# Two of three partial products in one matmul, in the products that end in the residual

## The chip, the core and the metric

The program runs on one core of a Trainium2 chip. The metric is the device time of one execution, from the first to the last instruction and what little lies around them, in microseconds; three timed runs of the kernel before are known.

## The reference, cut to what matters

Two transformer blocks on 256 tokens of width 1024, everything in float32. The first block has two layers, each of a gated FFN, a mixer and another gated FFN; the second block has a hybrid mixer (a recurrence and latent attention), attention to a memory, and an FFN with a convolution. Cut to the statements whose last product ends in the residual `x`:

```python
for l in range(DEPTH):                                   # DEPTH = 2
    x = x + 0.5 * gate * swiglu(adaln_in(x, ...), w1, w3, w2)      # (silu(h @ w1) * (h @ w3)) @ w2, w2: 2752 x 1024
    h = adaln_in(x, ...) @ w_in[l]
    mix = mixer_ab(h, ...) if l % 2 == 0 else mixer_cd(h, ...)
    x = x + gate * (mix @ w_out[l])                      # w_out: 1024 x 1024
    x = x + 0.5 * gate * swiglu(adaln_in(x, ...), w1, w3, w2)
...                                                      # second block: hybrid mixer, then
x = x + memory_attention(...) @ w_mem_o                  # 512 x 1024
x = x + ffn(...) @ w_down                                # 2816 x 1024
```

Each `adaln_in` is a root-mean-square norm of `x` with a gain and a shift that come from a conditioning vector.

## The kernel before, in words

Features lie on partitions: `x` is [128, 8, 256], eight tiles n of 128 features by 256 tokens (T = 256). A float32 product is made of three products in a rounded format (fp32r), as both factors are split into a hi part and a lo part: hi·hi, hi·lo and lo·hi. For one block of 128 by 128 weights that is `mm3` (L649): three matmuls of 256 columns (258 where two columns for the shift are taken along, L1006 and its like), each with its own weight load, the first two with the weights' hi part on the operand's hi and lo part, the third with the weights' lo part on the operand's hi part. All three add up in one half of a PSUM bank.

Weights come as a stream of slabs [128, 1024] in a fixed order (`load_job`, queue of SyncE). ScalarE makes a slab's hi part (`hi_job`), VectorE its lo part (`lo_job`, L586, 128x1024); VectorE also makes the modulation's vectors from slabs of another kind in the same stream (an operation on 128x1024 that the profile calls CUSTOM_DVE_ANT_0, and `order` ISA). Five pairs of buffers hold hi and lo slabs.

`block_mms` (L691) runs through a stream of blocks, all K tiles of one output tile n in a row; it makes the last product of the four gated FFNs (22 K tiles; the 22nd has 64 rows with the hi and lo part in one tile, two matmuls), of the memory attention (4 K tiles) and of the last FFN, `ffn2` (22 K tiles). `slab_mms` (L665) takes a slab for each output tile (8 K tiles); it makes all first products and the mixers' output products. Output tiles rotate over three PSUM banks (`mmr`).

When an output tile is whole, `residual` (L901) runs on VectorE: one operation reads the 256 columns in PSUM, multiplies by the gate (or only adds) and adds to `x[:, n]`; then the bank is free. It also starts what the next norm needs of the tile (`Norm.feed`): ScalarE makes the hi part of gain times x and VectorE the lo part (`scale`), ScalarE squares the tile and VectorE adds the square to a sum (`square`). After the eighth tile two plain matmuls reduce the sum over partitions (`Norm.root`), eight small VectorE operations make the reciprocal root, and two matmuls against the identity spread it to all partitions. Where the next norm has a shift, one small VectorE operation (128x16, `shift_cols`) writes two extra columns of the operand, once the last tile of `x` is done.

The order of instructions on each engine is made while the program is written: `Sched` (L328) keeps a rough clock of every engine from fixed costs and always emits the step that could start first by these clocks; the engines then run strictly in this order. So every operation that is added or made shorter can move others past each other.

Of the kernel before, what the change touches and what calls it, by code (L numbers as in the profile page):

```python
# [12 lines left out]
F32R = mybir.dt.float32r  # L13
# [17 lines left out]
# (name, columns) of the per-channel vectors, one column per tile of 128 channels  # L31
# [17 lines left out]
# square constant matrices [128, 128]  # L49
# [3 lines left out]
def _shape_constants():  # L53
# [14 lines left out]
    # the head that each of 128 rows belongs to: tiles 0-3 hold two heads of 64 rows; tiles 4 and 5 four  # L68
    # heads of 32 rows in the order 0, 2, 1, 3
# [65 lines left out]
# groups of four slabs of the modulation's weights whose products run on the tensor engine, as nothing else does then  # L135
PE_GROUPS = (2,)
# order in which the modulation's nine sections are made
# [163 lines left out]
# how many slabs of the modulation's weights go with each slab of the stream's first stages  # L301
RATES = [(43, 0.55), (65, 0.7), (91, 0.5), (156, 0.31), (199, 0.5), (221, 0.75), (247, 0.4), (10 ** 6, 0.2)]
STAGES = (65, 91, 156, 221, 247, 312, 343, 351)
# other priorities in a stage of the stream
# [5 lines left out]
# Every engine runs its instructions in the order in which they are emitted. The parts of the program are  # L310
# generators ("jobs") that ask for an engine before each step, for events that other jobs fire and for tiles out of
# rings; the scheduler keeps a rough clock of every engine and always emits the step that can start first.
# [18 lines left out]
class Sched:  # L331
# [16 lines left out]
    # runs a job up to its next wait for an engine, an event or a ring  # L348
# [43 lines left out]
    # early: what an engine does before it waits for the operands  # L392
    def charge(self, e, cost, early=0.0, cols=0.0):
# [9 lines left out]
        if e == "pe":  # L403
            # the tensor engine's clock is full in a window after one in which enough columns left the array
            w = int(s / 3.4133)
            if self.busy.get(w - 1, 0.0) < 3060.0:
                cost *= 2
            for i in range(w, int((s + cost) / 3.4133) + 1):
                part = (min(s + cost, (i + 1) * 3.4133) - max(s, i * 3.4133)) / cost
                self.busy[i] = self.busy.get(i, 0.0) + part * cols  # L410
# [64 lines left out]
def _body(tc, ins, out, ctx, dbg=None):  # L475
# [78 lines left out]
    # a load in the order of the stream: the event fires at the time when it should have arrived  # L554
# [61 lines left out]
    # four slabs of the modulation as a row of 512, then as columns  # L616
# [31 lines left out]

    def mm3(ps, w, c, mh, ml, first, last):  # L649
# [13 lines left out]
    # products of whole slabs (K = 1024, one output tile each) with a shared moving operand. The first slabs go  # L663
    # through the parts of K side by side, as the operand may not be whole yet.
    def slab_mms(n, mh, ml, cols, done, kev, parts=(range(7), (7,)), dst=None, pen=None):  # L665
        s = 0
        while s < n:
            g = min(n, 3) if s == 0 else 1
            held = []
            for pi, part in enumerate(parts):  # L670
                for j in range(g):
# [5 lines left out]
                    for k in part:  # L677
# [6 lines left out]
                        mm3(ps[:, o:o + cols], w, k, mh[:, k, :cols], ml[:, k, :cols], first, last)  # L684
# [5 lines left out]
    # products of a stream of [128, 128] blocks, the K tiles of one output tile in a row  # L690
    def block_mms(outs, mh, ml, done, kev, pen=0.0, both=None):  # L691
        w, t = None, 0
        for n, ks in outs:
            ps, = yield mmr, 1
            for k in ks:
# [6 lines left out]
                if k == both:  # L702
                    for i in range(2):
                        pe.matmul(ps[:, :T], w[i][:, t % 8 * P:t % 8 * P + P], mh[:, k, :T], start=False, stop=(i == 1))
                else:
# [5 lines left out]
    # products with the tokens of the operand on partitions: parts [K tile, slab, first column] of 512 columns  # L711
# [17 lines left out]
    # hi and lo parts of a tile  # L729
# [9 lines left out]
    # r = (s / width + eps) ** -0.5: a seed y from the exponent's bits (within 3.5%), then the polynomial of  # L739
    # a = v y^2 that is 1 / sqrt(a) to 3e-8 there. Its leading factor is taken into v.  # L740
# [27 lines left out]
    # a column per token tile onto all partitions  # L768
# [10 lines left out]
    # the products run on A x (hi and lo parts); the root is multiplied in after them  # L779
    class Norm:  # L780
# [23 lines left out]
        # a tile that is normalised before the products  # L804
# [9 lines left out]
        # after the last use of the root its tile goes back  # L814
# [86 lines left out]
    def residual(n, ps, gate, nx):  # L901
        yield "dve"
        if gate is None:
            dve.tensor_tensor(x[:, n], ps[:, :T], x[:, n], ALU.add)
        else:
            dve.scalar_tensor_tensor(x[:, n], ps[:, :T], gate[:, n:n + 1], x[:, n], ALU.mult, ALU.add)
# [12 lines left out]
    # the root's product and the shift's product of an output tile  # L919
# [11 lines left out]
    def ffn(l, i, nm, nxt):  # L931
        with tc.tile_pool(name=f"ffn{l}{i}", bufs=1) as sp:
            gh = tl(sp, [P, 22, T], F32R)
            gl = tl(sp, [P, 21, T], F32R)
# [4 lines left out]
            # the products themselves if the operand was normalised, else with the root's product  # L939
            def done(s, ps):  # L940
# [10 lines left out]
                if s == 42:  # L951
# [9 lines left out]
                    # the last 64 rows' hi and lo parts share a tile; their weights are there twice  # L961
# [1370 lines left out]
```

## Time and profile before

| | us |
|---|---|
| three timed runs | 1434.87, 1426.93, 1431.79 |
| median | 1431.79 |
| profiled execution, span | 1425.3 |
| TensorE busy, weight loads busy | 1374.9, 1293.0 |
| VectorE busy | 1142.6 |
| ScalarE busy | 777.5 |
| DMA queue q1, share of 16 engines | 64.4% |

Of the profiled execution only the span is given; the median of the timed runs lies 6.5 us above it, the fastest 1.6 us. How to read the page: engines run side by side, so busy times don't add up to the span; matmuls are pipelined, so the time between two starts is what a matmul costs, not its duration; the chain of waits (part 4) says what the end waited for, step by step. Nearly every instruction is issued by one helper (L443), so rows are told apart by shapes and by place in time, not by line.

Places in time (us from the span's start), read from the timeline: last product of the first FFN 188 to 250, of the second 484 to 544, of the third 671 to 732, of the fourth 980 to 1041; output product of the first mixer 329 to 356, of the second 818 to 852; of the memory attention 1218 to 1231; of the last FFN 1358 to 1421.5.

### The profile page before, as it was taken

Reading aid. Unit: us, or ns where it says so; the run is one execution under the profiler, and the core shown is the slowest. Engines: PE = TensorE matmul, PEld = TensorE weight load, DVE = VectorE, ACT = ScalarE, POOL = GpSimd, SP = SyncE. Lnnn points to the kernel's source line nnn. Section 1 sums busy time; section 2 is a strip of 40 time slices with the busy share of each in tenths; the row PEclk is TensorE's granted clock in tenths of the full one; section 3 lists DMA queues with packets and bytes.
Section 4 is the critical chain, followed back from the end, with each engine's and each line's share of the span. In section 5 each row is a group of like instructions: output and inputs, shape, how many; then the busy total and the mean of one; then the engine's idle time right before and its main releaser. Section 6 shows DMA issues by size and latency. Waiting matters only on the chain.

```text
span 1425.3 us, 26961 instructions
## 1 busy us (share of the span) xinstructions
PE 1374.9 (96%) x10726; PEld 1293.0 (91%) x10726; DVE 1142.6 (80%) x2183; ACT 777.5 (55%) x1434; POOL 40.2 (3%) x44
## 2 busy tenths in 40 slices
PE   4899999999999999999999999999999998999998
PEld 1499999878999999999998789999997778999998
DVE  5778788796888777888979879986577978799962
ACT  2365554474555544555446646655455765676642
POOL 5200000000000000000000001000000000000000
PEclk9899999999999999999999999999999999999999
DMA  8679899754777787888984447776643134356671
GB/s 296 220 245 317 282 304 331 240 172 150 246 260 245 241 253 226 294 275 270 345 295 149 155 143 228 225 249 188 194 148 119 61 133 133 104 185 186 186 225 49
DMA packets 84656, 305.26 MB, mean 214 GB/s; under 512 B 9515, under 2 KB 11147, under 8 KB 84274
## 3 DMA queue, kind: packets, MB, share of 16 engines
q1 hardware_dynamic: 83250, 299.31, 64.4%
q0 software_dynamic: 1280, 4.22, 0.8%
q8 instruction: 84, 1.38, 0.4%
q14 instruction: 42, 0.34, 0.1%
HBM read 302.43 MB, written 1.06 MB: 213 GB/s over the span
## 4 chain that ended last, share of the span: by engine, by line
PE 83%; DVE 9%; ACT 4%; DMA 2%; issue 1%; POOL 1%; SPq 0%; ACTq 0%; DVEq 0%; POOLq 0%
PE u L443 83%; DVE u L443 9%; ACT u L443 4%; DMA u<-wst 1%; POOL u L443 1%; DMA u<-x 1%; ACT L443 0%; SPq L556 0%; POOL u L2138 0%; ACTq L443 0%; DVEq L443 0%; DVE u L1642 0%; DVE u L1145 0%; DVE u L1643 0%; DVEq L1145 0%
## 5 line engine op out<-in xcount | busy, mean ns | idle before, releaser
L443 PE MATMUL u<-u,u 128*128 128x258 f32 (+7 forms) x10724 | 1373.8, 292 | 46.6 <-ACT u L443 25.5
L443 PEld LDWEIGHTS u<-u,u 128*128 128x128 f32 (+3 forms) x10724 | 1292.8, 189 | 126.7 <-issue 49.9
L443 ACT ACTIVATE u<-u 128x1024 fp32r<-128x1024 f32 (+6 forms) x1001 | 602.8, 632 | 537.4 <-PE u L443 317.3
L443 DVE TENSOR_TENSOR u<-u,u 128x1024 fp32r<-128x1024 f32 (+5 forms) x1065 | 734.5, 721 | 183.4 <-ACT u L443 92.9
L443 DVE SCALAR_TENSOR_TENSOR u<-u,u,u 128x256 f32<-128x256 f32 (+2 forms) x393 | 185.7, 481 | 63.3 <-PE u L443 32.7
L443 ACT ACTIVATE u<-u,u 128x256 f32<-128x256 f32 (+2 forms) x323 | 165.2, 523 | 84.0 <-DVE u L443 61.6
L443 DVE CUSTOM_DVE_ANT_0 u<-u,u,u 128x1024 f32<-128x1024 f32 x140 | 179.7, 1286 | 4.2 <-ACT u L443 3.6
L443 DVE SCALAR_TENSOR_TENSOR u<-u,u 128x2 f32<-128x2 f32 (+5 forms) x127 | 32.5, 261 | 13.3 <-ACT u L443 5.6
L443 ACT ACTIVATE u<-u,u,u 128x256 f32<-128x256 f32 (+1 forms) x43 | 23.8, 564 | 8.3 <-DVE u L443 5.7
L443 DVE TENSOR_SCALAR u<-u,u 128x256 f32<-128x256 f32 (+1 forms) x80 | 25.9, 370 | 1.0 <-ACT u L443 0.2
L443 DVE TENSOR_SCALAR u<-u 128x2 f32<-128x2 f32 (+9 forms) x82 | 14.9, 184 | 7.4 <-PE u L443 3.8
L443 DVE TENSOR_REDUCE u<-u 128x2 f32<-128x512 f32 x20 | 13.3, 685 | 2.0 <-PE u L443 2.0
L443 ACT ACT_TABLE_LOAD x11 | 14.1, 1283 | 0.9 <-PEq L2309 0.7
L443 POOL TENSOR_TENSOR u<-u,u 128x256 f32<-128x256 f32 (+1 forms) x10 | 14.0, 1405 | 13.3 <-ACT u L443 13.0
L1325 POOL DMA_DIRECT2D u<-rope x1 | 0.6, 556 | 479.7 <-PE u L443 479.7
L443 POOL TENSOR_SCALAR u<-u 64x256 f32<-64x256 f32 (+2 forms) x12 | 12.4, 1036 | 25.0 <-DVE u L443 18.8
L443 DVE DVE_READ_ACCUMULATOR2_ANT u<- 128x1 f32 x156 | 12.7, 82 | 0.0
L443 ACT ACTIVATION_READ_ACCUMULATOR u<-u,u,u 128x1 f32 x40 | 8.1, 204 | 0.0
L443 DVE TENSOR_TENSOR u<-u 128x2 f32<-128x2 f32 (+5 forms) x36 | 6.7, 188 | 0.6
L1139 POOL DMA_DIRECT2D u<-sel x1 | 0.6, 575 | 194.0 <-DMA u<-mst 194.0
L443 DVE CUSTOM_DVE_ANT_0 u<-u,u 128x256 f32<-128x256 f32 x16 | 6.0, 419 | 0.0
L443 DVE TENSOR_TENSOR_SCAN u<-u,u 128x256 f32<-128x256 f32 x8 | 5.5, 682 | 0.0
(35 smaller groups left out, 25.8 us busy)
## 6 DMA issues: line engine op xcount, KB each, us to landing
u<-wst SPq DMA_DIRECT2D x417, 512.0 KB, 4.5
u<-mst SPq DMA_DIRECT2D x144, 512.0 KB, 4.8
u<-u POOLq DMA_DIRECT2D x1, 1536.0 KB, 11.8
u<-x SPq DMA_DIRECT2D x1, 1024.0 KB, 8.6
u<-mem SPq DMA_DIRECT2D x1, 1024.0 KB
u<-lruw POOLq DMA_DIRECT2D x2, 512.0 KB, 4.3
out<-u SPq DMA_DIRECT2D x8, 128.0 KB, 2.7
u<-decay SPq DMA_DIRECT2D x1, 512.0 KB, 9.3
```

The source lines that it names most:

```text
L443: r = f(*args, **kw)
L1139: nc.gpsimd.dma_start(sel, ins["sel6"][:8, :4 * P])
L1325: nc.gpsimd.dma_start(rope, ins["rope"])
```

## The change

Operand tiles of the eight products named above are allocated as one tile that holds hi and lo parts side by side (`parts`). A new `mm3_wide` takes the place of `mm3` there: one matmul of 512 columns has the weights' hi part on the operand's hi and lo parts, and writes both halves of the PSUM bank; a second one of 256 columns adds the weights' lo part on the operand's hi part to the first half. `residual` then adds both halves to `x`, in two operations. The 22nd K tile of the gated FFNs keeps its two matmuls, and the hybrid mixer's output product keeps `mm3`. The lo tile of the gated FFNs has 22 tiles instead of 21. The diff also takes comments out; they are left out here.

```diff
+    joined = {}
+
+    def parts(pool, n, cols=T):
+        t = tl(pool, [P, 2, n, cols], F32R)
+        h, lo = t[:, 0], t[:, 1]
+        joined[id(h)] = t, h
+        return h, lo
+
+    def mm3_wide(ps, w, c, mh, k, first, last):
+        h, lo = w[0][:, c * P:(c + 1) * P], w[1][:, c * P:(c + 1) * P]
+        pe.matmul(ps.rearrange("p (a b) -> p a b", a=2), h, joined[id(mh)][0][:, :, k, :T], start=first, stop=False)
+        pe.matmul(ps[:, :T], lo, mh[:, k, :T], start=False, stop=last)
...
-                        mm3(ps[:, o:o + cols], w, k, mh[:, k, :cols], ml[:, k, :cols], first, last)
+                        if wide:
+                            mm3_wide(ps, w, k, mh, k, first, last)
+                        else:
+                            mm3(ps[:, o:o + cols], w, k, mh[:, k, :cols], ml[:, k, :cols], first, last)
...
+                elif wide:
+                    mm3_wide(ps, w, t % 8, mh, k, k == ks[0], k == ks[-1])
...
-    def residual(n, ps, gate, nx):
+    def residual(n, ps, gate, nx, wide=False):
         yield "dve"
-        if gate is None:
-            dve.tensor_tensor(x[:, n], ps[:, :T], x[:, n], ALU.add)
-        else:
-            dve.scalar_tensor_tensor(x[:, n], ps[:, :T], gate[:, n:n + 1], x[:, n], ALU.mult, ALU.add)
+        for p in (ps[:, :T], ps[:, T:])[:1 + wide]:
+            if gate is None:
+                dve.tensor_tensor(x[:, n], p, x[:, n], ALU.add)
+            else:
+                dve.scalar_tensor_tensor(x[:, n], p, gate[:, n:n + 1], x[:, n], ALU.mult, ALU.add)
+        if gate is not None:
...
-            gh = tl(sp, [P, 22, T], F32R)
-            gl = tl(sp, [P, 21, T], F32R)
+            gh, gl = parts(sp, 22)
...
-                                 lambda n, ps: residual(n, ps, gate, nx), kev, both=21)
+                                 lambda n, ps: residual(n, ps, gate, nx, True), kev, both=21, wide=True)
```

The same two edits (`parts`, and `wide=True` with `residual(..., True)`) stand in both mixers, in the memory attention and in `ffn2`.

What it does to the order on the engines. On TensorE, at the start of the first FFN's last product (u_178 and u_179 are the operand's hi and lo part, u_88 and u_89 a slab's hi and lo part, u_129 a PSUM bank):

```order
 L443 MATMUL u_128<-u_69,u_86 128x258
 L443 MATMUL u_128<-u_68,u_87 128x258
-L443 MATMUL u_129<-u_178,u_88 128x256
-L443 MATMUL u_129<-u_179,u_88 128x256
+L443 MATMUL u_129<-u_178,u_88 128x512
 L443 MATMUL u_129<-u_178,u_89 128x256
```

One row of three goes in each such group; TensorE has 10204 rows before and 9196 after. Nothing else of TensorE's order changes but the places of some reductions and spreads at the ends of the stages. The farthest is at the end of the first mixer, where the reduction of the sum of squares (u_135<-u_65,u_93) stands among the first products of the next FFN (u_68 and u_69 are its operand; u_130, u_128 and u_129 its first three output tiles), before:

```order
L443 MATMUL u_128<-u_68,u_86 128x258
L443 MATMUL u_128<-u_69,u_86 128x258
L443 MATMUL u_128<-u_68,u_87 128x258
L443 MATMUL u_135<-u_65,u_93 128x1 x2
L443 MATMUL u_128<-u_68,u_86 128x258
L443 MATMUL u_128<-u_69,u_86 128x258
L443 MATMUL u_128<-u_68,u_87 128x258
```

and after:

```order
L443 MATMUL u_130<-u_68,u_84 128x258
L443 MATMUL u_130<-u_69,u_84 128x258
L443 MATMUL u_130<-u_68,u_85 128x258
L443 MATMUL u_135<-u_65,u_93 128x1 x2
L443 MATMUL u_130<-u_68,u_84 128x258
L443 MATMUL u_130<-u_69,u_84 128x258
L443 MATMUL u_130<-u_68,u_85 128x258
```

Before, 36 matmuls of the next FFN stand ahead of the reduction (21 into u_130, 15 into u_128); after, 18. In the same way the reduction stands 12 matmuls earlier at the end of the third FFN, 6 earlier at the end of the second mixer, 9 later at the end of the fourth FFN and 15 later at the end of the memory attention. On VectorE at the end of the first mixer (u_67 is x, u_69 and u_68 the next operand's lo and hi part, u_93 the sum of squares, u_121 the gate; the row 128x8x2 writes the shift's columns, the rows 128x1024 make lo slabs), before:

```order
L443 SCALAR_TENSOR_TENSOR u_67<-u_128,u_121,u_67 128x256
L443 SCALAR_TENSOR_TENSOR u_67<-u_129,u_121,u_67 128x256
L443 TENSOR_TENSOR u_69<-u_70,u_68 128x8x2
L443 TENSOR_TENSOR u_87<-u_76,u_86 128x1024
L443 SCALAR_TENSOR_TENSOR u_69<-u_67,u_122,u_68 128x256
L443 TENSOR_TENSOR u_93<-u_93,u_101 128x256
L443 SCALAR_TENSOR_TENSOR u_69<-u_67,u_122,u_68 128x256
L443 TENSOR_TENSOR u_89<-u_80,u_88 128x1024
L443 TENSOR_TENSOR u_93<-u_93,u_102 128x256
L443 TENSOR_TENSOR u_91<-u_81,u_90 128x1024
```

and after:

```order
L443 SCALAR_TENSOR_TENSOR u_67<-u_129,u_121,u_67 128x256 x2
L443 TENSOR_TENSOR u_69<-u_70,u_68 128x8x2
L443 TENSOR_TENSOR u_87<-u_76,u_86 128x1024
L443 SCALAR_TENSOR_TENSOR u_69<-u_67,u_122,u_68 128x256
L443 TENSOR_TENSOR u_93<-u_93,u_94 128x256
L443 SCALAR_TENSOR_TENSOR u_69<-u_67,u_122,u_68 128x256
L443 TENSOR_TENSOR u_93<-u_93,u_101 128x256
L443 SCALAR_TENSOR_TENSOR u_69<-u_67,u_122,u_68 128x256
L443 TENSOR_TENSOR u_93<-u_93,u_102 128x256
L443 TENSOR_TENSOR u_89<-u_80,u_88 128x1024
```

The last residual operation of the stage is a pair, the shift's columns come behind it, and three scales and three additions, in place of two and two, now stand between the shift and the small operations of the root; one of the two lo slabs that stood between them has moved behind the root.

## Rows read from the trace of the kernel before

**Rows 1.** Page: busy time (part 1), granted clock (part 2), chain by engine (part 4)
```profile
PE 1374.9 (96%) x10726; PEld 1293.0 (91%) x10726; DVE 1142.6 (80%) x2183; ACT 777.5 (55%) x1434; POOL 40.2 (3%) x44
...
PEclk9899999999999999999999999999999999999999
...
PE 83%; DVE 9%; ACT 4%; DMA 2%; issue 1%; POOL 1%; SPq 0%; ACTq 0%; DVEq 0%; POOLq 0%
```

**Rows 2.** Groups by form, whole span: count | busy us, mean ns | idle before, releaser
```profile
L443 PE MATMUL u<-u,u 128*128 128x258 f32 x4992 | 628.4, 285 | 11.6 <-DVE u L443 6.2 <-ACT u L443 5.3
L443 PE MATMUL u<-u,u 128*128 128x256 f32 x4976 | 624.9, 287 | 10.8 <-ACT u L443 5.8 <-DVE u L443 4.7
```

**Rows 3.** Timeline of TensorE, four stretches: start us, duration us, instruction, count
```profile
189.73 59.52 PE L443 MATMUL u<-u,u 128*128 128x256 f32 x504
...
489.79 50.44 PE L443 MATMUL u<-u,u 128*128 128x256 f32 x431
...
1221.74 9.52 PE L443 MATMUL u<-u,u 128*128 128x256 f32 x78
...
1357.75 63.74 PE L443 MATMUL u<-u,u 128*128 128x256 f32 x530
```

**Rows 4.** The same view of 512 columns, and their group by form
```profile
1155.38 1.33 PE L443 MATMUL u<-u,u 128*128 128x512 f32 x5
...
L443 PE MATMUL u<-u,u 128*128 128x512 f32 x5 | 1.3, 396 | 0.0
```

**Rows 5.** Timeline of TensorE where one column follows each weight load
```profile
1143.26 1.48 PE L443 MATMUL u<-u,u 128*128 128x1 f32 x12
```

**Rows 6.** Timeline of VectorE, the residual after the first mixer; plain additions later
```profile
341.19 2.26 DVE L443 SCALAR_TENSOR_TENSOR u<-u,u,u 128x256 f32<-128x256 f32 x5 [7.32 <-PE u L443]
...
1226.59 1.08 DVE L443 TENSOR_TENSOR u<-u,u 128x256 f32<-128x256 f32 x3
```

**Rows 7.** Stretches, all engines: PE, PEld, DVE, ACT, POOL busy us, PEclk, DMA share
```profile
188.30:249.80 61.50, 61.50 (x523) 61.33 (x521) 52.92 (x77) 30.17 (x41) 0.00 (x0) 1.00 0.93 324
341.00:357.80 16.80, 15.12 (x129) 14.83 (x127) 14.40 (x27) 11.56 (x21) 0.00 (x0) 1.00 0.45 141
836.90:853.40 16.50, 15.28 (x128) 14.79 (x126) 13.99 (x27) 12.86 (x23) 0.54 (x1) 1.00 0.54 165
...
1221.00:1234.40 13.40, 13.40 (x113) 13.38 (x112) 10.95 (x30) 10.20 (x20) 0.00 (x0) 1.00 0.13 40
```

**Rows 8.** Timeline at the end of the first FFN
```profile
249.88 0.48 DVE L443 SCALAR_TENSOR_TENSOR u<-u,u,u 128x256 f32<-128x256 f32 x1
...
250.28 0.17 DVE L443 TENSOR_TENSOR u<-u,u 128x16 fp32r<-128x16 f32 x1
...
250.50 0.39 PE L443 MATMUL u<-u,u 128*128 128x258 f32 x1 [0.66 <-DVE u L443]
```

**Rows 9.** Timeline at the end of the first mixer
```profile
353.97 0.49 DVE L443 SCALAR_TENSOR_TENSOR u<-u,u,u 128x256 fp32r<-128x256 f32 x1 [1.70 <-ACT u L443]
...
357.05 0.87 DVE L443 SCALAR_TENSOR_TENSOR u<-u,u,u 128x256 f32<-128x256 f32 x2
...
357.83 1.30 DVE L443 TENSOR_TENSOR u<-u,u 128x16 fp32r<-128x16 f32 x2
...
358.06 0.39 PE L443 MATMUL u<-u,u 128*128 128x258 f32 x1 [1.94 <-DVE u L443]
```

**Rows 10.** The same, VectorE behind it; TensorE by form in 362.3 to 362.9
```profile
360.18 2.69 DVE L443 TENSOR_TENSOR u<-u,u 128x1024 fp32r<-128x1024 f32 x3
362.88 0.16 DVE L443 TENSOR_SCALAR u<-u 128x2 f32<-128x2 f32 x1
...
L443 PE MATMUL u<-u,u 128*128 128x1 f32 x4 | 0.5, 230 | 0.0
```

**Rows 11.** Timeline at the end of the second mixer
```profile
852.31 0.48 DVE L443 SCALAR_TENSOR_TENSOR u<-u,u,u 128x256 fp32r<-128x256 f32 x1 [1.50 <-ACT u L443]
...
853.66 0.39 PE L443 MATMUL u<-u,u 128*128 128x258 f32 x1 [0.53 <-DVE u L443]
...
855.05 0.42 DVE L443 TENSOR_TENSOR u<-u,u 128x256 f32<-128x256 f32 x1
...
856.72 0.16 DVE L443 TENSOR_SCALAR u<-u 128x2 f32<-128x2 f32 x1
```

**Rows 12.** Timeline at the end of the fourth FFN
```profile
1042.52 0.42 DVE L443 TENSOR_TENSOR u<-u,u 128x256 f32<-128x256 f32 x1
...
1042.99 0.38 PE L443 MATMUL u<-u,u 128*128 128x1 f32 x2 [0.71 <-DVE u L443]
```

**Rows 13.** Timeline, the last tile
```profile
1421.52 0.42 DVE L443 TENSOR_TENSOR u<-u,u 128x256 f32<-128x256 f32 x1 [7.49 <-PE u L443]
1421.97 0.33 SPq L917 DMA_DIRECT2D out<-u  x1
```

More of the change, by code (lines that the diff above doesn't have):

```diff
@@ L661, in take, with slab_mms @@
         return hl_t.pop(i)
-    def slab_mms(n, mh, ml, cols, done, kev, parts=(range(7), (7,)), dst=None, pen=None):
+    def slab_mms(n, mh, ml, cols, done, kev, parts=(range(7), (7,)), dst=None, pen=None, wide=False):
         s = 0
@@ L688, in slab_mms, with block_mms @@
             s += g
-    def block_mms(outs, mh, ml, done, kev, pen=0.0, both=None):
+    def block_mms(outs, mh, ml, done, kev, pen=0.0, both=None, wide=False):
         w, t = None, 0
@@ L1126, in mixer_ab @@
         with tc.tile_pool(name="ab", bufs=1) as sp:
-            mh = tl(sp, [P, 8, T], F32R)
-            ml = tl(sp, [P, 8, T], F32R)
+            mh, ml = parts(sp, 8)
             kev = [Event() for _ in range(8)]
@@ L1300, in mixer_ab @@
             nx = yield from nxt()
-            yield from slab_mms(8, mh, ml, T, lambda n, ps: residual(n, ps, gate, nx), kev,
+            yield from slab_mms(8, mh, ml, T, lambda n, ps: residual(n, ps, gate, nx, True), kev, wide=True,
                                 parts=((4, 5, 6, 7, 0, 1, 2), (3,)))
@@ L1308, in mixer_cd @@
         with tc.tile_pool(name="cd", bufs=1) as sp:
-            mh = tl(sp, [P, 8, T], F32R)
-            ml = tl(sp, [P, 8, T], F32R)
+            mh, ml = parts(sp, 8)
             kev = [Event() for _ in range(8)]
@@ L1502, in mixer_cd @@
             nx = yield from nxt()
-            yield from slab_mms(8, mh, ml, T, lambda n, ps: residual(n, ps, gate, nx), kev,
+            yield from slab_mms(8, mh, ml, T, lambda n, ps: residual(n, ps, gate, nx, True), kev, wide=True,
                                 parts=((0, 1, 2, 3), (4, 5, 6), (7,)))
@@ L1979, in memory_attention @@
             q4 = [tl(sp, [P, T]) for _ in range(4)]
-            oh = tl(sp, [P, 4, T], F32R)
-            ol = tl(sp, [P, 4, T], F32R)
+            oh, ol = parts(sp, 4)
             prs, pts = ring(sp, 4, [P, 2 * T]), ring(sp, 4, [P, 2, T])
@@ L2067, in memory_attention @@
             yield from block_mms([(n, range(4)) for n in range(8)], oh, ol,
-                                 lambda n, ps: residual(n, ps, None, nx), kev)
+                                 lambda n, ps: residual(n, ps, None, nx, True), kev, wide=True)
             put(sm, nm.cols)
@@ L2073, in ffn2 @@
         with tc.tile_pool(name="ffn2", bufs=1) as sp:
-            gh = tl(sp, [P, 22, T], F32R)
-            gl = tl(sp, [P, 22, T], F32R)
+            gh, gl = parts(sp, 22)
             up = ring(sp, 4, [P, T + 2])
@@ L2113, in last @@
             def last(n, ps):
-                yield from residual(n, ps, None, None)
+                yield from residual(n, ps, None, None, True)
                 fin.append(n)
@@ L2119, in ffn2 @@
             all_out = Event()
-            yield from block_mms([(n, range(22)) for n in range(8)], gh, gl, last, kev)
+            yield from block_mms([(n, range(22)) for n in range(8)], gh, gl, last, kev, wide=True)
             yield all_out
```

## The prediction

> **What bounds the kernel now.** I read first the page's busy times, its row of granted clocks and its sums along the chain of waits [rows 1]. TensorE is busy 96% of the span, 83% of the chain is its own work and 9% VectorE's; the clock is granted at the upper of its two levels in nearly every slice. So a microsecond counts if it is on TensorE, or if it is one for which TensorE waits.
>
> Next I read the groups by form [rows 2]. A mean of 285 to 287 ns is a duration, and matmuls overlap; what one costs is the time from start to start. The timeline gives that for unbroken rows of matmuls [rows 3]: less one overlap (0.28 us, the mean duration), divided by the count less one. The last product of the first FFN gives (59.52 - 0.28) / 503 = 117.8 ns, that of the second (50.44 - 0.28) / 430 = 116.6, of the memory attention (9.52 - 0.28) / 77 = 120.0, of `ffn2` (63.74 - 0.28) / 529 = 120.0. I use 117.2 for the gated FFNs and the mixers.
>
> Then the stretches [rows 7]. In the first FFN's last product TensorE is busy for all of 61.50 us, VectorE for 52.92; the DMA engines' share is 0.93. The output products of the two mixers differ: TensorE works 15.12 of 16.80 and 15.28 of 16.50 us, VectorE 14.40 and 13.99. There VectorE is nearly as full as TensorE, and an operation more has little room. The memory attention lies between (10.95 of 13.40).
>
> **TensorE's part.** 1008 matmuls go with their loads: 4 x 168 in the gated FFNs, 176 in `ffn2`, 32 in the memory attention, 2 x 64 in the mixers. In each triple, two steps of 256 columns become one of 512. Of 512 columns with a load each there are short rows: (1.33 - 0.396) / 4 = 233.5 ns [rows 4]. That is 0.456 ns a column, and 117.2 / 256 is 0.458: the step goes with the columns, and hardly anything is saved by having one instruction fewer. A step has a floor: a matmul of one column with its load takes (1.48 - 0.25) / 11 = 112 ns [rows 5]; the 0.25 is an estimate for the last one's own duration, whose kind takes 0.23 on the mean [rows 10]. It lies below 117.2, so I take the loads as covered already, and removing 1008 of them gives nothing by itself. A triple in the FFNs and mixers: 3 x 117.2 = 351.6 becomes 233.5 + 117.2 = 350.7; saved 0.9 x (672 + 128) = 0.7 us. In `ffn2` and the memory attention 3 x 120.0 = 360.0 becomes 353.5; saved 6.5 x 208 = 1.4 us. Together -2.1 us. The trace of before has no alternation of 512 and 256 columns, so bounds: nothing saved, if `ffn2`'s 120 is due to something else; 6.5 x 1008 = 6.6 us, if its difference holds everywhere. I take 2.1, the direct reading.
>
> The Trainium skill would have it faster. Its page "TensorE: Matmul & The Clock Gate", section "Back-to-back issue gap", says that in a stream of loads and matmuls both set the spacing, and gives about 81 ns at 128 columns and 131 at 512; estimated from these by a straight line, 256 columns would take 98 ns, a triple would go from 293 to 229 ns, and the kernel would gain 64 x 1008 = 65 us, to about 1370. The rows here, 117.2 at 256 and 233.5 at 512, disagree, and the measurement decides. The section's formula for a single matmul (columns / 2.4 + 2.5 ns: 109.2 and 215.8) is nearer; its difference, 2.5 ns for each matmul that goes, would be 2.5 us.
>
> **VectorE's part.** 64 operations are added, one for each output tile of 8 stages: 48 with a gate, 16 plain. Five with a gate in one row take 2.26 us [rows 6]; with 0.48 for one alone [rows 8] that is (2.26 - 0.48) / 4 = 0.44 from start to start; two take 0.87 [rows 9], 0.39 apart. I take 0.40. Three plain ones take 1.08 [rows 6]; with 0.42 for one, (1.08 - 0.42) / 2 = 0.33. So VectorE gets 48 x 0.40 + 16 x 0.33 = 24.5 us. Within a stage they lie in VectorE's idle time: a tile of the FFNs takes TensorE some 7.6 us, and VectorE has (61.50 - 52.92) / 8 = 1.07 us idle for each. Three banks rotate, so a bank that comes free 0.4 us later stops nothing. What stays is the end of each stage, where TensorE waits for the last tile. Behind the added operation on VectorE stand the shift's columns, and behind those TensorE's next product. Without that cover the price of all would be 24.5 us.
>
> - Ends of the first three FFNs. Residual at 249.88, shift at 250.28, TensorE at 250.50 after a gap of 0.66 that VectorE ends [rows 8]. The added operation goes straight into that gap: 3 x 0.40 = +1.2.
> - End of the fourth FFN. No shift follows; TensorE waits 0.71 for the sum of squares [rows 12]. Its reduction now stands 9 matmuls later, 9 x 0.12 = 1.07 us of work that fills the gap, while the sum comes 0.40 later: 0.71 + 0.40 - 1.07 leaves 0.04, so -0.6, between -0.7 and +0.4.
> - End of the first mixer. VectorE does eight residuals more, 3.2 us. The last falls in the stage's end in any case; of the other seven, 2.8 us, VectorE has 16.80 - 14.40 = 2.40 idle in the stretch, 1.70 of it just before 353.97, waiting for ScalarE [rows 7, 9]. So 0.3 to 0.4 of these is not covered; with the last one 0.7. But part of the gap of 1.94 ahead of TensorE [rows 9] is a chain through ScalarE that the operations can run beside, so I take +0.3 (between 0 and 3.2).
>  After that comes the reduction. It now stands 18 matmuls, 18 x 0.12 = 2.2 us, earlier, and one scale and one addition more stand ahead of it, one lo slab fewer. Before, the sum was whole in time: the last addition lies in a row of three from 360.18 to 362.87, and the 128x1 matmuls ran after 362.3 without a wait [rows 10]. After, the sum is whole once shift and one lo slab (1.30 together [rows 9]), three scales and three additions (3 x 0.40 + 3 x 0.33 = 2.2) have run, 3.5 us after the shift's start. TensorE starts 0.23 after that (358.06 against 357.83) and reaches the reduction 18 x 0.12 = 2.2 us later, at 2.4. It stalls for about 1.1 us. This is a new wait; behind it in TensorE's order stand all further products. +1.1, between 0 and 2.
> - End of the second mixer. VectorE had 2.5 us idle, 1.50 of it in the one gap before 852.31, TensorE's own gap was 0.53, and the addition of the squares came at 855.05 with the root at 856.72 [rows 7, 11]. With the reduction 6 matmuls (0.7 us) earlier: +0.1 for the tile and +0.65 for the reduction, between 0 and 3.
> - Memory attention. 8 x 0.33 = 2.7 us against 13.40 - 10.95 = 2.45 idle; the reduction is 15 matmuls later, so it waits for nothing: +0.2, between -0.2 and +0.5.
> - Last tile. One addition of 0.42 stands between TensorE's last matmul and the store [rows 13]: +0.33 and no cover.
>
> Sum: 1.2 - 0.6 + 1.4 + 0.75 + 0.2 + 0.33 = +3.3 at the ends, -2.1 on TensorE: +1.2. The profiled span of 1425.3 us becomes about 1426.5. The median of the timed runs lies 6.5 us above that span, so I forecast 1433 us. What a measurement of this kernel tells from no change is about 0.5%, 7.2 us.
>
> **Rivals.**
>
> A, faster: the loads do cost, and the 512 columns hide the next one. For it: weight loads are busy 91% of the span [rows 1], the floor of 112 ns lies only 5 ns under the step of 117.2, and `ffn2` runs at 120. If the 256 behind a 512 comes down by those 5 ns and the 512 by the 6.5 that `ffn2` shows, the saving is 11.5 x 1008 = 11.6 us, less 3.3: 1425.3 - 8.3 = 1417, as a median 1423.5. Against it: 512 columns with a load each, whose load has twice the time to hide in, still take 0.456 ns a column [rows 4]. In the first FFN a gain of over 7% would also meet the DMA, whose share is 0.93. Chance 0.17.
>
> The Trainium skill speaks for A: "Perfetto Trace Analysis", section "Identifying the Most-Contended Engine", judges TensorE's headroom by the busy share of weight loads and not by that of matmuls. By that share of 91%, removing 1008 loads would count by itself; the rows of 512, where loads are half as many, show no gain from it.
>
> B, slower: at the ends of the mixers VectorE is the bound, and the idle time of rows 9 and 11 cannot be used, since it waits for ScalarE's operands and strict order puts the added operations behind the wait. Then the eight added residuals come in full, 8 x 0.40 = 3.2 us in each mixer, the reductions stall 1.5 us each, the FFN ends add 1.2, the rest 0.5: 6.4 + 3.0 + 1.7 = 11.1, and TensorE gives nothing back: 1425.3 + 11.1 = 1436.4, as a median 1443. It decides once less than about half of the 2.4 us idle takes added work. For it: VectorE is 86% busy there, and other work there is needed by TensorE too. Against it: 1.70 us of the idle time lies late, where residuals may run ahead. Chance 0.15.
>
> C: the change doesn't do what it says, since a matmul of 512 columns over two separated pieces runs as two with a load each. Then TensorE saves nothing and the ends stay: 1428.6, as a median 1435. Rows 4 were rows of 512 without such a cut; nothing else speaks for it. Chance 0.08.
>
> **How the numbers follow.** Forecast 0.60 at 1433, with its own range of 1427 to 1438; A 0.17 at 1423.5, B 0.15 at 1443, C 0.08 at 1435. Range: 1421 to 1443, which leaves out the far part of A and B's upper half. Faster by over 0.5% is below 1424.6: most of A, 0.14. Slower by over 0.5% is above 1439: B, and a little of the forecast, 0.18. Within: 0.68.
>
> **What would show it.** In the changed kernel's profile: (1) the pace of the alternating rows; near 351 ns a triple confirms the TensorE part, 340 or less speaks for A. (2) The gap ahead of TensorE at the end of the first FFN, 0.66 before, now near 1.06. (3) At the end of the first mixer a new wait of TensorE on the reduction near 1.1 us, and the gap of 1.94 hardly longer; a gap of 4 or more speaks for B. (4) VectorE's busy time up by about 24.5 us, its share of the chain hardly. (5) No wait on the reduction at the end of the fourth FFN. Wrong would be the whole if the pace of triples lies off by 10 ns, which is 10 us, or if VectorE delays the lo slabs inside a stage.

## The result: about 0.8% slower, and the profile after

| | before | after |
|---|---|---|
| timed runs | 16 | 16 |
| median, us | 1431.99 | 1442.29 |
| lowest to highest, us | 1426.93 to 1437.84 | 1436.10 to 1454.13 |
| ratio of after to before | | 1.0078, 95% interval 1.0063 to 1.0093 |
| profiled execution, span, us | 1425.3 | 1442.8 |
| mean granted clock in it | 0.986 | 0.975 |

The forecast was 1433 us and no change that can be told; the change is slower by more than 0.5%. The median lies just inside the stated range of 1421 to 1443, at the edge that was rival B's time. First the page of the changed kernel: busy time, granted clock in forty slices, the chain by engine.

```profile
PE 1384.6 (96%) x9718; PEld 1255.8 (87%) x9718; DVE 1170.7 (81%) x2247; ACT 778.2 (54%) x1434; POOL 38.7 (3%) x44
...
PEclk9899999999999999999999999999998999899999
...
PE 83%; DVE 9%; ACT 4%; DMA 1%; POOL 1%; issue 1%; SPq 0%; ACTq 0%; DVEq 0%; POOLq 0%
```

Against [rows 1]: TensorE has 1008 matmuls fewer and yet is busy 10 us longer; the row of clocks shows two digits under 9 that it did not have. VectorE has 28 us more (24.5 were worked out).

The groups by form, as in [rows 2], and one stretch of `ffn2` from the timeline (as in [rows 3]):

```profile
L443 PE MATMUL u<-u,u 128*128 128x256 f32 x2960 | 549.7, 292 | 5.7 <-DVE u L443 5.2 <-ACT u L443 0.5
L443 PE MATMUL u<-u,u 128*128 128x512 f32 x1094 | 386.5, 402 | 7.0 <-DVE u L443 6.9
```

```profile
1379.80 57.59 PE L443 MATMUL u<-u,u 128*128 128x512 f32 x331
```

2016 matmuls of 256 columns have become 1008 of 512. In `ffn2` the row of 331 matmuls begins and ends with one of 512 columns, so 165 pairs lie between the two starts: (57.59 - 0.39) / 165 = 347 ns a pair (0.39 us is the mean duration of one of 512 columns there), where the triple took 360 ([rows 3], 3 x 120.0) and 353.5 were forecast.

**Two parts of the time.** Each run has its span and its mean granted clock. Span times clock is what the run would take, roughly, had the clock never fallen; the rest is lost to the clock. The split is a rough one: within a kernel the first part scatters by 1.1 to 2.5 us from run to run, and it is lower in runs that lost more. Over the 208 runs of the table, each kernel's mean taken out, a microsecond that is called lost goes with 0.77 us of span, not with 1. Means, with the standard error over the runs (ratios are to the runs of before in the same set; the 79 runs of before are those of the three later sets, without one slow run of 2654.81 us):

| kernel | runs | span x clock, us | lost to the clock, us | ratio to before (interval) |
|---|---|---|---|---|
| before | 79 | 1404.8 ± 0.2 | 25.2 ± 0.5 | |
| after, first set | 16 | 1409.3 ± 0.5 | 31.5 ± 1.2 | 1.0078 (1.0063 to 1.0093) |
| after, second set | 6 | 1410.3 ± 0.6 | 36.9 ± 1.8 | 1.0131 (1.0109 to 1.0152) |
| TensorE's part alone | 12 | 1402.4 ± 0.6 | 22.9 ± 1.5 | 0.9976 (0.9960 to 0.9992) |
| VectorE's part alone | 11 | 1411.2 ± 0.4 | 27.6 ± 1.6 | 1.0057 (1.0033 to 1.0080) |
| only the mixers | 10 | 1410.5 ± 0.6 | 29.7 ± 1.4 | 1.0061 (1.0039 to 1.0083) |
| all but the mixers | 12 | 1403.1 ± 0.4 | 30.5 ± 0.7 | 1.0021 (1.0005 to 1.0038) |
| last tiles as before | 12 | 1405.7 ± 0.7 | 28.2 ± 1.4 | 1.0033 (1.0011 to 1.0054) |
| all but the third FFN | 6 | 1408.4 ± 0.4 | 32.7 ± 0.8 | 1.0069 (1.0050 to 1.0087) |
| only the third FFN | 12 | 1406.6 ± 0.7 | 28.5 ± 2.1 | 1.0029 (1.0005 to 1.0053) |
| FFNs, seven tiles | 12 | 1402.6 ± 0.7 | 28.5 ± 2.2 | 1.0001 (0.9974 to 1.0028) |
| FFNs but the third, seven tiles | 8 | 1401.2 ± 0.9 | 22.1 ± 1.5 | 0.9939 (0.9915 to 0.9962) |
| the same again | 12 | 1401.0 ± 0.7 | 24.8 ± 0.8 | 0.9970 (0.9952 to 0.9987) |

Over both sets of after, 4.8 us are direct (1409.6 against 1404.8) and 7.8 us are clock (33.0 against 25.2). Counted at 0.77, the clock's share is 7.8 x 0.77 = 6.0 us, and 6.6 are direct. So of the 12.6 us, 4.8 to 6.6 are direct and 6.0 to 7.8 are clock. The forecast had +1.2 for the first and nothing for the second.

**Where the direct part is.** At the same place of the program both kernels have put the same number of columns through TensorE, so two traces can be laid beside each other by that number. The delay of after grows and shrinks like this (us; both traces of after, and their low-clock stretches named):

| place | first | second |
|---|---|---|
| last products of the first, second, third and fourth FFN | -0.24, -0.44, -0.51, -0.49 | -0.22, -0.50, -0.51, -0.51 |
| `ffn2` | -2.2 | -2.2 |
| ends of the first and second FFN | +0.57, +0.42 | +0.57, +0.36 |
| end of the third FFN, at most 1.7 of it clock | +3.4 | +3.2 |
| end of the fourth FFN | -0.1 | -0.1 |
| first mixer's output product and end | +2.4 | +2.4 |
| second mixer's, in the first trace with 6.8 us at the lower clock | +4.0 | +1.6 |
| memory attention and end, clock in both | +2.7 | +1.4 |
| the part of it behind the low clock | +0.6 | +0.6 |

In the second mixer the kernel before itself lost 1.7 us to a low clock at 828 that neither trace of after has. From the last residual of the stage on (854 to 862 us of before) the delay grows by 4.9 in the first trace and by 2.5 in the second, with the same work: the 6.8 us at the lower clock cost 2.4 us, not 3.4. So the direct part there is 3.3 in both. Without the clock, and with 0.47 for the last tile (below), the rows add up to some +5 us.

**The end of the first FFN** (timeline: start, duration, instruction, idle time before it), beside [rows 8]:

```profile
249.05 0.48 DVE L443 SCALAR_TENSOR_TENSOR u<-u,u,u 128x256 f32<-128x256 f32 x1
...
249.57 0.48 DVE L443 SCALAR_TENSOR_TENSOR u<-u,u,u 128x256 f32<-128x256 f32 x1
249.97 1.30 DVE L443 TENSOR_TENSOR u<-u,u 128x16 fp32r<-128x16 f32 x2
...
250.19 0.64 PE L443 MATMUL u<-u,u 128*128 128x258 f32 x3 [1.18 <-DVE u L443]
```

The added operation stands between, and TensorE's gap is 1.18 for 0.66.

**The end of the third FFN**, first before, then after:

```profile
728.85 2.55 DVE L443 TENSOR_TENSOR u<-u,u 128x1024 fp32r<-128x1024 f32 x2
...
731.86 0.48 DVE L443 SCALAR_TENSOR_TENSOR u<-u,u,u 128x256 f32<-128x256 f32 x1 [0.46 <-issue]
...
732.26 0.17 DVE L443 TENSOR_TENSOR u<-u,u 128x16 fp32r<-128x16 f32 x1
...
732.48 0.63 PE L443 MATMUL u<-u,u 128*128 128x258 f32 x3 [0.57 <-DVE u L443]
```

```profile
737.09 1.28 DVE L443 CUSTOM_DVE_ANT_0 u<-u,u,u 128x1024 f32<-128x1024 f32 x1
...
738.32 0.48 DVE L443 SCALAR_TENSOR_TENSOR u<-u,u,u 128x256 f32<-128x256 f32 x1
...
738.84 0.48 DVE L443 SCALAR_TENSOR_TENSOR u<-u,u,u 128x256 f32<-128x256 f32 x1
739.24 0.17 DVE L443 TENSOR_TENSOR u<-u,u 128x16 fp32r<-128x16 f32 x1
...
739.46 0.58 PE L443 MATMUL u<-u,u 128*128 128x258 f32 x1 [2.18 <-DVE u L443]
```

Before, two lo slabs end, VectorE idles 0.46 us and takes the last residual at once. After, a modulation operation of 1.28 us (the CUSTOM row) stands directly ahead of it, and the pair starts when that ends. TensorE's gap is 2.18 for 0.57. The changed kernel's order has it there; with the third FFN left as before, it goes back (last experiments).

**The first mixer**, beside [rows 7, 9]: VectorE's row of additions, TensorE's gaps, and the stretch.

```profile
343.90 3.62 DVE L443 SCALAR_TENSOR_TENSOR u<-u,u,u 128x256 f32<-128x256 f32 x8 [5.82 <-PE u L443]
...
344.96 14.13 PE L443 MATMUL u<-u,u 128*128 128x512 f32 x80 [0.41 <-DVE u L443]
...
359.32 0.38 PE L443 MATMUL u<-u,u 128*128 128x258 f32 x1 [0.23 <-ACT u L443]
...
361.47 1.30 DVE L443 TENSOR_TENSOR u<-u,u 128x16 fp32r<-128x16 f32 x2
...
361.69 2.31 PE L443 MATMUL u<-u,u 128*128 128x258 f32 x17 [1.99 <-DVE u L443]
...
365.02 0.27 PE L443 MATMUL u<-u,u 128*128 128x1 f32 x1 [1.02 <-DVE u L443]
```

```profile
343.90:361.70 17.80, 15.17 (x86) 12.78 (x84) 17.52 (x35) 13.37 (x24) 0.00 (x0) 1.00 0.52 178
```

VectorE is busy 17.52 of 17.80 us: the idle time of before is used up. TensorE waits at four points: 0.41 for a bank (three tiles end together and their pairs stand in one row on VectorE), 0.23 and 1.99 at the end (1.94 before), and 1.02 for the reduction, the new wait that was forecast at 1.1.

**The second mixer**, its first matmul and second weight load before, and then the stretch in the second trace of after, where the clock did not fall behind it:

```profile
827.21 0.42 ACT L443 ACTIVATE u<-u 128x256 fp32r<-128x256 f32 x1 [10.23 <-DVE u L443]
827.66 0.42 DVE L443 TENSOR_TENSOR u<-u,u 128x256 fp32r<-128x256 f32 x1 [0.48 <-ACT u L443]
...
827.68 0.38 PE L443 MATMUL u<-u,u 128*128 128x256 f32 x1 [1.80 <-ACT u L443]
...
828.14 6.03 PEld L443 LDWEIGHTS u<-u,u 128*128 128x128 f32 x23 [0.27 <-DVE u L443]
```

```profile
838.61 0.42 ACT L443 ACTIVATE u<-u 128x256 fp32r<-128x256 f32 x1 [10.23 <-DVE u L443]
839.05 0.42 DVE L443 TENSOR_TENSOR u<-u,u 128x256 fp32r<-128x256 f32 x1 [0.48 <-ACT u L443]
...
839.53 0.50 PE L443 MATMUL u<-u,u 128*128 128x512 f32 x1 [2.30 <-DVE u L443]
...
847.97 0.50 PE L443 MATMUL u<-u,u 128*128 128x512 f32 x1 [0.41 <-DVE u L443]
...
862.72 0.38 PE L443 MATMUL u<-u,u 128*128 128x258 f32 x1 [0.61 <-ACT u L443]
...
864.23 1.97 PE L443 MATMUL u<-u,u 128*128 128x258 f32 x14 [1.12 <-DVE u L443]
...
866.83 4.17 PE L443 MATMUL u<-u,u 128*128 128x1 f32 x33 [0.63 <-DVE u L443]
...
869.09 1.28 DVE L443 CUSTOM_DVE_ANT_0 u<-u,u,u 128x1024 f32<-128x1024 f32 x1
...
870.37 1.22 DVE L443 TENSOR_TENSOR u<-u,u 128x1024 fp32r<-128x1024 f32 x1
...
871.64 1.57 PE L443 MATMUL u<-u,u 128*128 128x258 f32 x11 [0.65 <-DVE u L443]
...
873.90 2.51 PE L443 MATMUL u<-u,u 128*128 128x128 f32 x19 [0.44 <-DVE u L443]
```

At the stage's start, TensorE before goes on when ScalarE has made the hi part (gap 1.80); the matmul of 512 columns needs the lo part too, which VectorE makes 0.45 us later (2.30). This costs hardly anything, because before the second matmul waits for the same lo part (its weight load starts at 828.14, behind VectorE): matched by columns, TensorE is only 0.06 us later at the third product, in both traces. At the end, two waits were in no step of the prediction. A lo slab that TensorE needs next (870.37 to 871.59) stands behind a modulation operation of 1.28 us; TensorE goes on 0.05 us after its end, having waited 0.65. And the spread of the root (the row 128x128) waits 0.44 for VectorE's small operations. With 0.41 for a bank, 0.63 for the reduction and 0.24 more at the end itself (0.61 and 1.12 for 0.96 and 0.53), the gaps add up to 2.4; before, TensorE waits only at the end itself. What else makes up the 3.3 is not broken down here.

**The end of the fourth FFN**, VectorE's next lo slab before, and then after, beside [rows 12]; **the end of the memory attention** and **the last tile**, after, beside [rows 13]:

```profile
1043.37 1.23 DVE L443 TENSOR_TENSOR u<-u,u 128x1024 fp32r<-128x1024 f32 x1 [0.43 <-ACT u L443]
```

```profile
1053.31 1.22 DVE L443 TENSOR_TENSOR u<-u,u 128x1024 fp32r<-128x1024 f32 x1
...
1055.32 0.95 PE L443 MATMUL u<-u,u 128*128 128x1 f32 x6 [0.70 <-DVE u L443]
```

```profile
1252.43 0.47 DVE L443 SCALAR_TENSOR_TENSOR u<-u,u,u 128x256 fp32r<-128x256 f32 x1
...
1252.96 1.81 PE L443 MATMUL u<-u,u 128*128 128x256 f32 x13 [0.90 <-DVE u L443]
...
1438.59 0.89 DVE L443 TENSOR_TENSOR u<-u,u 128x256 f32<-128x256 f32 x2 [6.74 <-PE u L443]
```

At the fourth FFN's end the lo slab, which before came behind the sum of squares, now stands ahead of it, so TensorE still waits 0.70 for the sum (0.71 before), although its reduction comes 9 matmuls later. At the memory attention's end TensorE waits 0.90 for the last tile's lo part, a wait that before does not have. The last tile's additions take 0.89 us for 0.42.

**The clock.** TensorE's clock is granted at one of two levels, 1.00 or 0.50. Four stretches of after, and the first two's like of before:

```profile
278.00:281.40 3.40, 3.40 (x17) 1.99 (x17) 1.62 (x6) 0.00 (x0) 0.00 (x0) 1.00 0.51 178
281.60:291.60 10.00, 10.00 (x38) 6.71 (x37) 7.18 (x26) 1.71 (x3) 0.00 (x0) 0.50 0.33 107
739.00:742.20 3.20, 2.74 (x12) 2.74 (x13) 2.75 (x7) 1.34 (x3) 0.00 (x0) 0.50 0.98 367
861.90:868.50 6.60, 6.60 (x32) 6.45 (x32) 2.83 (x9) 2.33 (x7) 0.00 (x0) 0.50 0.55 181
```

```profile
278.30:281.70 3.40, 3.40 (x17) 1.98 (x16) 1.65 (x6) 0.00 (x0) 0.00 (x0) 1.00 0.62 182
281.90:291.90 10.00, 10.00 (x75) 8.26 (x74) 9.45 (x33) 5.40 (x11) 0.00 (x0) 1.00 0.40 109
```

In the first row of each, both kernels do the same work at the same pace, 17 matmuls in 3.40 us; behind it the clock falls in one and not in the other, 38 matmuls for 75 in 10 us. Nothing of the change lies there.

### The profile page after: what moved, and what is told of

Its sections match the earlier page's. It is cut to its first block, busy times and chain, and to the rows that moved or that the text cites. A ratio compares the mean times of both kernels' runs of the same rounds, so it can differ in the third digit from the quotient of the medians.

```text
span 1442.8 us, 24990 instructions
## 1 busy us (share of the span) xinstructions
PE 1384.6 (96%) x9718; PEld 1255.8 (87%) x9718; DVE 1170.7 (81%) x2247; ACT 778.2 (54%) x1434; POOL 38.7 (3%) x44
## 4 chain that ended last, share of the span: by engine, by line
PE 83%; DVE 9%; ACT 4%; DMA 1%; POOL 1%; issue 1%; SPq 0%; ACTq 0%; DVEq 0%; POOLq 0%
PE u L443 83%; DVE u L443 9%; ACT u L443 4%; POOL u L443 1%; DMA u<-mem 1%; DMA u<-x 1%; ACT L443 0%; DMA u<-wst 0%; SPq L556 0%; POOL u L2155 0%; ACTq L443 0%; DVEq L443 0%; DVE u L2095 0%; DVE u L1661 0%; DVE u L1165 0%
## 5 line engine op out<-in xcount | busy, mean ns | idle before, releaser
L443 PE MATMUL u<-u,u 128*128 128x258 f32 (+6 forms) x9716 | 1383.6, 307 | 53.9 <-DVE u L443 27.3
L443 PEld LDWEIGHTS u<-u,u 128*128 128x128 f32 (+2 forms) x9716 | 1255.5, 190 | 180.9 <-issue 53.1
L443 DVE TENSOR_TENSOR u<-u,u 128x1024 fp32r<-128x1024 f32 (+4 forms) x1081 | 740.1, 716 | 172.1 <-ACT u L443 82.9
L443 DVE SCALAR_TENSOR_TENSOR u<-u,u,u 128x256 f32<-128x256 f32 (+2 forms) x441 | 208.7, 482 | 58.3 <-ACT u L443 30.0
L443 POOL TENSOR_TENSOR u<-u,u 128x256 f32<-128x256 f32 (+1 forms) x10 | 14.4, 1438 | 12.6 <-ACT u L443 12.3
```

Of the source, the lines that this page charges most:

```text
L443: r = f(*args, **kw)
```

## The experiments

Theory 1: the added operations make TensorE wait, and the clock falls behind such waits. Theory 2: the clock falls by chance. Theory 3: the matmuls of 512 columns bring it down. Theory 4, from the last set of runs on: the order at the third FFN's end does.

**The changed kernel again**, no edit.

> The changed kernel once more, for a second trace. Theory 1 (the ends: the added VectorE operations lengthen TensorE's waits at the ends of the stages, and the clock falls behind them): 1.006 to 1.009 of before, and the low-clock stretches stand again behind the same ends (third FFN near 739 us, second mixer near 862). Theory 2 (the place where the clock falls is chance, and the kernel before only had it fall less often): the stretches stand elsewhere than in the first trace, the mean clock is spread as widely as in the runs of before, and before's clock is lower than 0.986 in most of its runs.

Slower than in the first set, in the clock part alone, and above the range of theory 1. Theory 2 has something for it: before's clock lies under 0.986 in 16 of the set's 23 runs. The low-clock stretch behind the third FFN stood again (740.1 to 743.5); the one behind the second mixer did not.

**TensorE's part alone.**

```diff
-        for p in (ps[:, :T], ps[:, T:])[:1 + wide]:
+        for p in (ps[:, :T],):
```

> TensorE's part alone: the matmul of 512 columns stays, but the residual adds only the first half; the product of the weights' hi part with the operand's lo part is left out of x. Theory 1: 3 to 5 us faster than before (0.997), clock near before's. Theory 2: between 0.997 and 1.007, with low-clock stretches in any place. Theory 3: 1.003 or more, clock near 0.978.

Faster than before, 2.4 us in span times clock and the clock part no greater. Theory 3 falls, and the saving was of the size forecast.

**The last tile of each stage as before.**

```diff
-                        if wide:
+                        if wide and s + j < n - 1:
...
-                elif wide:
+                elif wide and n < 7:
...
-        for p in (ps[:, :T], ps[:, T:])[:1 + wide]:
+        for p in (ps[:, :T], ps[:, T:])[:1 + (wide and n < 7)]:
```

> The change in the first seven output tiles of each stage; the eighth keeps three matmuls of 256 columns and one addition, so nothing is added behind TensorE's last matmul. Theory 1: most of the loss is gone, 0.997 to 1.001 of before, clock near before's. Theory 2 or 3: 1.004 to 1.008, as the changed kernel.

In between. Taking the added operation away from the very end gave back 3.9 us of the direct part, but the other seven pairs still fill VectorE in the mixers, and the modulation operation still stands ahead of the third FFN's last residual (TensorE's gap there 1.85).

**VectorE's part alone.**

```diff
-        pe.matmul(ps.rearrange("p (a b) -> p a b", a=2), h, joined[id(mh)][0][:, :, k, :T], start=first, stop=False)
+        t = joined[id(mh)][0]
+        if first:
+            pe.matmul(ps.rearrange("p (a b) -> p a b", a=2), h, t[:, :, k, :T], start=True, stop=False)
+        else:
+            pe.matmul(ps[:, :T], h, t[:, 0, k, :T], start=False, stop=False)
+            pe.matmul(ps[:, T:], h, t[:, 1, k, :T], start=False, stop=False)
```

> VectorE's part alone: behind the first K tile of each output tile the matmul of 512 columns is issued as two of 256, one into each half of the bank; the two additions stay. Take a run's time in two parts: its span times the mean granted clock (before 1405.1, changed kernel 1409.6 us), and the rest, lost to the lower clock (before 24.0, changed 33.0). Theory 1 (the added operations make TensorE wait at the ends, and the clock falls behind such waits): span times clock 1412 to 1415, lost 30 or more, in all 1.011 to 1.016 of before. Theory 3 (matmuls of 512 columns bring the clock down): lost near 24, in all 1.006 at most.

The direct part is +6.4, a little under theory 1's; the clock part, +2.4 ± 1.7, is less than it wants, so the ratio missed; it is where theory 3 put it, which had fallen with TensorE's part. With that part, -2.4, the direct parts add up to +4.0, against +4.8 for the whole change. In neither of these two runs does the modulation operation hold up the third FFN's last residual (TensorE's gap there is 1.09 here and 0.57 in the other), so the sum leaves that cost out. A form that split the first K tile too gave no result.

**All but the mixers**, and **only the mixers**: `wide=True` and `residual(..., True)` taken out of the mixers, or of everything else.

> The change everywhere but in the two mixers' output products, which stay as before. Theory 1: the mixers' ends make up some 5.5 of the 9 us of waits, so span times clock is 1404 to 1405 and lost 26 to 29: 1.001 to 1.004 of before. Theory 2 (the clock falls by chance, with no tie to the ends): lost 31 to 37 as in the changed kernel, 1.004 to 1.008.

> The kernel before with the change in the two mixers' output products alone. By the traces their ends cost 2.4 and 3.2 us of wait: span times clock 1410 to 1411. Theory 1: lost 29 to 31, in all 1.006 to 1.009 of before. Theory 4: lost 24 to 27, 1.003 to 1.005.

The direct parts are -1.7 and +5.7; the clock parts +5.3 and +4.5. All of the direct loss is the mixers'; the clock is lost with and without them. Only the mixers came out as theory 1 says. Without them the ratio is in theory 1's range too, but more clock was lost than it allows.

**The FFNs alone, first seven tiles**, and **the same without the third FFN** (twice).

```diff
-                                 lambda n, ps: residual(n, ps, gate, nx, True), kev, both=21, wide=True)
+                                 lambda n, ps: residual(n, ps, gate, nx, (l, i) != (1, 0)), kev, both=21, wide=(l, i) != (1, 0))
```

> The change only in the four gated FFNs and the last FFN, and there only in the first seven output tiles; mixers, memory attention and every eighth tile stay as before. At the end of the third FFN one modulation operation of VectorE still stands ahead of the last residual. Theory 1: TensorE's saving of about 3.5 us, less 1.2 at the third FFN's end: span times clock 1402 to 1403, lost 24 to 26, 0.997 to 1.000 of before. Theory 2: lost 28 or more, 1.001 to 1.006.

> As the one before, with the third FFN as in the kernel before too, by which the modulation operation stands behind the last residual again; the version that should beat both kernels. Theory 1: span times clock 1401 to 1402.5, lost 22 to 25, 0.996 to 0.999 of before. Theory 2: lost 28 or more, 1.000 to 1.005.

> The fastest version once more, for a second set of times: the change in the first seven output tiles of the first, second and fourth FFN and of the last FFN. If its saving is TensorE's alone: span times clock 1401 to 1402, lost 24 to 26, in all 0.996 to 0.998 of before. If the first set stands: 0.992 to 0.996.

The second kernel is faster than before in both sets and beats both kernels: 3.6 and 3.8 us in span times clock, and no more clock lost than before. The first set's ratio was lower than forecast, the second's as forecast for TensorE's saving alone. Its gap at the third FFN's end is before's (start, duration, instruction, idle time):

```profile
730.20 5.08 PE L443 MATMUL u<-u,u 128*128 128x258 f32 x40 [0.57 <-DVE u L443]
```

Where the third FFN takes part, 1.4 to 1.6 us of the direct gain are gone; whether the clock too could not be told (28.5 ± 2.2).

**The third FFN alone**, and **all but it**.

> The kernel before with the change in the third FFN alone. Theory 4: span times clock about 1 us over before's, lost 28 to 31 against 25, in all 1.002 to 1.005 of before. Theory 1: 1 us of wait and 1 us of clock, 1.001 to 1.002. Theory 2: lost as before, 1.000 to 1.001.

> The changed kernel with its third FFN as before, by which the modulation operation stands behind that FFN's last residual again. Time split as above (span times clock; lost to the lower clock). Theory 4 (the order at the third FFN's end is what brings the clock down more often, there and shortly behind): lost 25 to 28, near before's, span times clock near 1408, in all 1.002 to 1.005 of before. Theory 1 (any wait brings it down, in proportion): lost 30 to 32, 1.005 to 1.008. Theory 2 (chance): lost 31 to 36 as in the changed kernel, 1.007 to 1.011.

Alone it costs 1.8 us directly, in all 0.3%, as theory 4 has it. But taking it out of the changed kernel leaves the clock part where it was (32.7). Theory 4 falls.

**What the traces say of the clock's place.** Behind the second mixer's end, rows as above, in two of the kernels whose mixers have two additions (only the mixers, then all but the third FFN) and in two others (all but the mixers, then the FFNs but the third):

```profile
857.90:864.50 6.60, 6.60 (x32) 6.45 (x31) 3.02 (x9) 1.52 (x4) 0.00 (x0) 0.50 0.62 182
```

```profile
872.70:875.90 3.20, 3.20 (x15) 3.20 (x16) 3.00 (x11) 0.00 (x0) 0.00 (x0) 0.50 0.85 292
```

```profile
858.00:878.00 20.00, 18.22 (x149) 17.60 (x148) 17.79 (x43) 12.63 (x26) 0.54 (x1) 1.00 0.74 251
```

```profile
856.00:878.00 22.00, 21.56 (x180) 21.35 (x180) 20.86 (x47) 13.37 (x27) 4.63 (x4) 1.00 0.71 233
```

Within 14 us behind that end there is a low-clock stretch in five of the six traces of kernels whose mixers have two additions (not in the second of after) and in none of the seven of the others. In three of the five it begins at a wait of 2.1 to 2.5 us, 9 to 13 us behind the end, where three kernels with unchanged mixers wait 0.4 to 0.8. At this place theory 1 is borne out, though the same kernel can do without the low clock. At the third FFN's end it is not: the low clock is there in both traces of the whole change and in no other, although five other kernels wait 1.1 to 2.3 us there. Elsewhere, matched by columns, the stretches of all thirteen traces stand at much the same places of the program, in kernels of both kinds: near 57, 282 or 334, 829, 1075 to 1095, 1114, 1175 and 1207 us of before, among others. Which of them fall differs from trace to trace; the one near 282 is there in seven, the one near 334 in the other six. Over all kernels, those that add waits lost 2 to 12 us more to the clock, some of them within the noise, and those that add none (TensorE's part alone, the FFNs without the third) lost no more than before; but the loss is not in proportion to the waits. So the second addition brings the loss, as the run without it shows (22.9 for 33.0); how a wait of a microsecond or two brings the clock down in one execution and not in the next stays open, and so does why the kernel without changed mixers loses 5.3 us more.

## Why the prediction was wrong

**TensorE's saving: right in sign, too small in the trace.** Forecast -2.1. The stages add up to -3.9 by matching columns, -2.2 of it in `ffn2`, where 1.1 was forecast (6.5 x 176); by span times clock TensorE's part alone gives -2.4. That the step goes with the columns held: 347 / 768 = 0.452 ns a column.

**Ends of the FFNs: two right, one wrong, one right by luck.** +0.40 each was forecast; the first two measured +0.57 and +0.36 to +0.42, the third some +1.6 without clock (+2.1 in the trace of all but the mixers, where the clock did not fall there). The failed step is "the added operation goes straight into that gap": there the order had changed as well, which the changed kernel's order showed (the modulation operation ahead of the last residual) and the prediction did not look at. The fourth, -0.1 for -0.6, was within its bounds, but not for the reason given: the wait for the reduction did not go (0.70 for 0.71), because a lo slab had moved ahead of the sum of squares.

**First mixer: right in kind, short in size.** The reduction's wait was 1.02 for 1.1, the end +0.28 for +0.3. Missing were the wait for a bank, held off by "a bank that comes free 0.4 us later stops nothing" (true in the FFNs, where tiles end one by one, not where three end together), and some tenths in handing over; 2.4 for 1.4.

**Second mixer: the mis-sized term of the direct part.** +0.75 was forecast, 3.3 measured (with the mixers alone, 5.7 less the first's 2.4 is 3.3 too). The prediction priced the reduction (0.63 for 0.65), but not the lo slab that comes late behind it (0.65), the spread (0.44) or the bank (0.41).

**Memory attention and last tile: short in size.** +0.2 and +0.33 were forecast, +0.6 and +0.47 measured. The reduction waits for nothing there, as forecast; the first product behind the stage waits 0.90.

**The step that failed: waits were left out of the sum, and the clock was priced at nothing.** The prediction read "the upper of its two levels in nearly every slice" and took it for a constant. But before already loses 25.2 us a run to the lower level, and the changed kernel 7.8 more; at 0.77 that is 6.0, about half of the 12.6. The waits themselves were the other half: they cost some 9 us (about 5 direct and up to 3.9 saved), not 3.3. Priced directly alone, at 4.8 to 6.6 us, the result would still have been within 0.5%, 7.2 us.

**The rivals.** B came out at the right time, 1443, and its mechanism is the one seen in the first mixer: VectorE full, idle time gone. But its sum is not how the time came about: it had 9.4 us of waits at the mixers, 5.7 were measured, and the rest is clock; that it met the time is luck. A fell as a whole: TensorE gave back 2.4 to 3.9 us, not 11.6. In `ffn2`, though, a pair is 13 ns shorter than the triple, as much as A asked for (11.5); whether the loads cost there or something else was not told apart. C fell with the rows of 512 columns: their number is 1008 up.

## What to carry to other kernels

An operation that is added where an engine hands over is to be counted wherever that engine is nearly full, not only at the last tile, and the order around it is to be read anew at every end: at the third FFN's an instruction that had moved cost more than the one added, and at the fourth's one that had moved kept a wait that was to go. One matmul for two operands also waits for the later of the two, which costs nothing where the next matmul waited for it before. Split every run's time by the granted clock before looking for causes, and keep in mind that a stretch at half clock can cost less than half its length (here 2.4 of 6.8 us); and take such a change only where its cost is covered, as here in the FFNs' first seven tiles.

## What was not expected of the hardware

A kernel whose TensorE is busy 96% of the span still spends some 50 us a run at half clock (at most 25.2 us lost), and two executions of the same work lose the clock at partly different places. A matmul of 512 columns between two of 256 in `ffn2` makes a pair of 347 ns, less than 233.5 + 120.0 of the same widths apart.
